# Gate product on VectorE, block copies on three engines and a step ahead of the convolution, gate and value steps side by side, in a two-layer encoder trunk

## The chip, the core and the metric

The kernel runs on one core of a Trainium2 chip. The core has five engines that each work through a queue of their own in order: TensorE (PE, with its weight loads as PEld), VectorE (DVE), ScalarE (ACT), GpSimd (POOL) and SyncE (SP), which issues most transfers. The metric is the time of one execution on the device in microseconds (us); lower is better.

## What is computed

The input is 256 positions of 2048 features in float32. Two layers follow each other: a mixer (grouped-query attention in layer 0, dilated windowed attention in layer 1) and a gated MLP with a convolution of width 3 over the positions between up-projection and activation. The change lies in the MLP, and in one table for the second mixer that is prepared beside the first MLP.

```python
D_FF = 5632
CONV_WIDTH = 3

def conv_ffn(h, w_up, conv_w, conv_b, w_down):
    u = h @ w_up                                  # [256, 2 * D_FF]
    c = u.shape[-1]
    u = lax.conv_general_dilated(u, conv_w[:, None, :].astype(u.dtype), window_strides=(1,),
                                 padding=((1, 1),), dimension_numbers=('NWC', 'WIO', 'NWC'),
                                 feature_group_count=c) + conv_b
    gate, val = jnp.split(u, 2, axis=-1)
    return (jax.nn.silu(gate) * val) @ w_down

def reference(x, ...):
    h = x
    for i in range(DEPTH):                        # 2 layers
        hn = rms_norm(h, mix_norm[i])
        h = h + (mixer_a(hn, ...) if i % 2 == 0 else mixer_b(hn, ..., rel_bias))
        h = h + conv_ffn(rms_norm(h, ffn_norm[i]), w_up[i], conv_w[i], conv_b[i], w_down[i])
    return rms_norm(h, final_norm)
```

## The kernel before

**Matrix products.** Every weight block of 128 x 1024 is loaded into one of six `raw` slots by SyncE (`feed`, `load_raw`). ScalarE rounds it to `wh` (line 120) and VectorE forms the remainder `wl` (line 121); these pairs lie in a ring of three slots, and four in the down-projection. The activations are split in the same way. A product is then three matmuls, high by high, high by low and low by high (lines 145 to 147), each with 512 columns. One weight block feeds 12 matmuls. This is called a step here, because `step()` is called after it.

**The up-projection.** `ffn` cuts the 5632 hidden features into 11 blocks of 512, in two halves of 6 and 5 (`HALVES`). For block p the kernel projects the gate block and then the value block: 8 steps each, a pair of 16 steps. What follows a projection is a generator, `up_post`, which `start` puts on the list `pending`. Each `step()` advances the oldest one to its next `yield`, so that its instructions are recorded between the matmuls of the following projection. The scheduler of the programming layer then sets the order on each engine; `wh` and `wl` are given priority there (`AHEAD`).

`up_post` has these pieces. ScalarE takes the projection out of the accumulators, scaled (`s`, line 420), and VectorE transposes each 32 x 32 block in place (`t`, line 421). Sixteen copies of 32 partitions x 256 elements then bring the blocks to their places in `u` (lines 425 to 436), so that positions lie along the free dimension. The string `PLACE` names the engine of each copy: p is GpSimd, a is ScalarE, any other letter is VectorE. Copies into the same 32 partitions are kept in sequence by semaphores. The convolution of each half block is one ScalarE instruction (line 441) and two on VectorE (lines 445 and 447) for each 128 features. For a gate, Silu follows. For a value, `glu` multiplies gate and value (line 455) and splits the product into the operands `ah` and `al` of the down-projection (lines 270 and 271).

**Blocks with sums.** The down-projection treats block 0 and block 2 of the first half and block 0 of the second (`SKG`) with seven products for eight, and so needs sums of their quarters. For these, `glu_forms` takes the place of `glu`: the same product (line 463), then more sums and splits. There are 6 such pairs in the two layers, and 16 plain ones.

**The down-projection** of a half follows its up-projection at once; the last value's `up_post` is worked off in its first steps. Sums of weight blocks (line 222) are made on VectorE.

**Bias lines.** The generator `bias_lines` is put on the list `spare` in layer 0. Six times it forms a line of biases by a matmul, copies it to `lnt` (line 883, two slots) and writes it to a scratch tensor in device memory with four transfers, issued by SyncE (line 886). `spare` is advanced only when `pending` is empty.

Of the kernel before, what the change touches and what calls it, by code (L numbers as in the profile page):

```python
# [10 lines left out]
ALU = mybir.AluOpType  # L11
# [11 lines left out]
NRAW, NHL = 6, 3  # L23
SKG = ((0, 2), (0,))
ORDER = (1, 2, 5, 3, 7, 6, 4)
PLACE = "pappaappapappapa"
AHEAD = 45
NWARM = 11

# [2 lines left out]
def tile_encoder(ctx: ExitStack, tc: tile.TileContext, x, xT, w_a, w_ao, q_gain, k_gain, w_b, w_bo,  # L32
                 rel_bias, gains, w_up, conv, w_down, final_norm, rope, ident_c, onehot, out):
    nc = tc.nc
# [45 lines left out]
    pending, spare = [], []  # L80

    def start(gen):
        if next(gen, StopIteration) is not StopIteration:
            pending.append(gen)

    def step():
        while pending:
            if next(pending[0], StopIteration) is not StopIteration:
                return
            pending.pop(0)  # L90
        if spare and next(spare[0], StopIteration) is StopIteration:
            spare.pop(0)

    def drain(keep=0):
        while len(pending) > keep:
            step()
# [279 lines left out]
    def ffn(l, hT, ss_in, g_next, last, side=None):  # L376
        with tc.tile_pool(name=nm("wpool"), bufs=1) as wp, tc.tile_pool(name=nm("fpool"), bufs=1) as fp:
# [35 lines left out]
            def up_post(acc, n, cs, after=None):  # L413
                u = us.pop(0)
                us.append(u)
                yield
                s = fp.tile([P, 2, 512], F32, tag="s", name=nm("s"))
                t = fp.tile([P, 2, 512], F32, tag="t", name=nm("t"))
                for m in range(2):
                    nc.scalar.activation(s[:, m], acc[m], AF.Copy, scale=rstd[:, m:m + 1])  # L420
                    nc.vector.transpose(t[:, m], s[:, m])  # L421
                yield
                tv = t.rearrange("p m (j q c) -> p j m q c", j=4, q=4)
                uv = u.rearrange("p j (m t) -> p j m t", m=2)
                for i in range(16):
                    if i == 8:
                        yield
                    a, b = i // 4, (i // 4 + i) % 4
                    dst = uv[32 * b:32 * b + 32, :, :, 32 * a:32 * a + 32]
                    src = tv[32 * a:32 * a + 32, :, :, b]  # L430
                    if PLACE[i] == "p":
                        nc.gpsimd.tensor_copy(dst, src)  # L432
                    elif PLACE[i] == "a":
                        nc.scalar.activation(dst, src, AF.Copy)  # L434
                    else:
                        nc.vector.tensor_copy(dst, src)
                for hh in range(2):
                    yield
                    c = cs[hh]
                    for j in range(2):  # L440
                        nc.scalar.activation(halves(c[:, j]), halves(u[:, 2 * hh + j])[:, :, :P], AF.Identity,
                                             bias=tap(n, 2 * hh + j, 3), scale=tap(n, 2 * hh + j, 1))
                    for j in range(2):
                        cj, uj = halves(c[:, j]), u[:, 2 * hh + j]
                        nc.vector.scalar_tensor_tensor(cj, halves(uj[:, :NT])[:, ::-1], tap(n, 2 * hh + j, 0), cj,  # L445
                                                       ALU.mult, ALU.add)
                        nc.vector.scalar_tensor_tensor(cj, halves(uj[:, 1:NT + 1])[:, ::-1], tap(n, 2 * hh + j, 2), cj,  # L447
                                                       ALU.mult, ALU.add)
                    if after is None:
                        nc.scalar.activation(c, c, AF.Silu)  # L450
                    else:
                        yield from after(hh)

            def glu(cg, cv, slots, k0):
                nc.gpsimd.tensor_tensor(cv, cg, cv, ALU.mult)  # L455
                yield
                for j in range(2):
                    split(*slots[k0 + j], cv[:, j, :])
# [1 line left out]
            kept = {}  # L460

            def glu_forms(cg, cv, fm, hh):
                nc.gpsimd.tensor_tensor(cv, cg, cv, ALU.mult)  # L463
                yield

                def put(p, src):
# [30 lines left out]
            for hf, (p0, p1) in enumerate(HALVES):  # L497
# [3 lines left out]
                def new_form():  # L501
                    pool, k = next(tags)
                    return tuple(pool.tile([P, NT], F32R, tag=f"a{c}{k}", name=nm("a" + c)) for c in "hl")

                for p in range(p0, p1):
                    if p - p0 in SKG[hf]:
                        fm = forms[p - p0] = {f: new_form() for f in (1, 7, 2, 5, 4, 6, 3) + (0,) * hf}
# [63 lines left out]
                        eng.dma_start(out.rearrange("(p m) c -> m p c", m=2)[m, :, n * 512:(n + 1) * 512], hs)  # L571

                np_ = p1 - p0
                drain(1)
                wd = w_down[l][:, p0:p1]
                if last and hf == 1:
# [287 lines left out]
    def bias_lines(wp, lp):  # L864
        if True:
# [9 lines left out]
            for b in range(6):  # L875
                for _ in range(2):
                    yield
                c0, w = ((0, 512), (512, 256), (768, 256))[b // 2]
                t = ps_tile()
                nc.tensor.matmul(t[:, :w], lh[:, 4 * b:4 * b + 4, :].rearrange("p a r -> p (a r)"),  # L880
                                 oh[:, c0:c0 + w], start=True, stop=True)
                ln = lnt[:, b % 2]
                nc.vector.tensor_copy(ln[:, :w], t[:, :w])
                dst = scr0[4 * b:4 * b + 4] if b < 2 else scr1[4 * (b - 2):4 * (b - 2) + 4]
                for i in range(4):
                    nc.sync.dma_start(dst[:, 32 * i:32 * i + 32, :], ln[:, :w])

    def mixer_b(hT, ss_in):
        with tc.tile_pool(name="bpool", bufs=1) as bp:
# [219 lines left out]
```

## Time and profile before

| what | value |
|---|---|
| median of 3 runs | 2330.32 us (2327.9 to 2332.01) |
| the profiled execution | 2330.72 us, span of its instructions 2328.9 us |
| granted TensorE clock, mean | 0.996 |
| PE, PEld busy | 2278.9 us, 1859.0 us |
| DVE, ACT, POOL busy | 1667.5 us, 1366.7 us, 388.4 us |
| HBM traffic | 429.20 MB read, 187 GB/s over the span |

The busy time of an engine is the time in which at least one of its instructions ran. In the views quoted below, a row of stretches has start and end in us, length, busy time of each engine with its number of instructions in brackets, the granted TensorE clock, the busy share of the DMA engines and GB/s. A row of the timeline has start and length in us, engine, line, operation, output and input; in square brackets stands how long the engine was idle before it, and who ended that. A group row ends with busy us and mean ns of one, then the idle time before them. Durations of instructions in a row on one engine can overlap a little.

### The profile page before, as it was taken

To read this page: it belongs to the slowest core of one execution; us is meant where nothing else is said; L and a number is where in the kernel's file an instruction comes from. 1 tells how busy PE (TensorE), PEld (TensorE's weight loads), DVE (VectorE), ACT (ScalarE), POOL (GpSimd) and SP (SyncE) were. 2 spreads that over 40 slices of the span, in tenths; PEclk is the share of its full clock that TensorE was granted. 3 is DMA by queue.
4 is the path that set the end of the run, shared out by engine and by line. 5 is a ranking of instruction groups with operands and counts; after the bars stand their busy time and mean duration, and the time that the engine had idled before them with its cause. 6 is when DMAs were issued, how large, how long until landed. Compare 5 with 4: busy or idle time off the path is not lost.

```text
span 2328.9 us, 28808 instructions
## 1 busy us (share of the span) xinstructions
PE 2278.9 (98%) x10169; PEld 1859.0 (80%) x10169; DVE 1667.5 (72%) x2301; ACT 1366.7 (59%) x2022; POOL 388.4 (17%) x524
## 2 busy tenths in 40 slices
PE   9999999999999999999999999999999999999998
PEld 7788777787787887788888888878778878878876
DVE  6877867667876667878776876575776688676684
ACT  6565467666546766455454454445767655567653
POOL 2210023233002333010000000001323210133230
PEclk9999999999999999999999999999999999999999
DMA  8445555665565564666655555555555556555663
GB/s 298 153 136 163 183 172 182 202 222 164 196 220 178 192 199 152 218 219 198 195 177 174 179 190 164 179 190 194 171 181 191 186 190 209 190 179 191 200 208 127
DMA packets 125136, 437.37 MB, mean 188 GB/s; under 512 B 13904, under 2 KB 16720, under 8 KB 124992
## 3 DMA queue, kind: packets, MB, share of 16 engines
q1 hardware_dynamic: 122912, 429.84, 56.6%
q0 software_dynamic: 1648, 5.15, 0.7%
q8 instruction: 79, 1.29, 0.2%
q14 instruction: 65, 0.53, 0.1%
q10 hardware_dynamic: 432, 0.56, 0.1%
HBM read 429.20 MB, written 6.29 MB: 187 GB/s over the span
## 4 chain that ended last, share of the span: by engine, by line
PE 72%; DVE 12%; POOL 7%; ACT 4%; issue 3%; DMA 3%; SPq 0%; DVEq 0%; POOLq 0%; ACTq 0%
PE acc L146 20%; PE acc L147 19%; PE acc L145 19%; DVE wl L121 5%; POOL u L432 4%; PE acc L258 4%; PE acc L253 3%; PE acc L255 3%; ACT wh L120 2%; POOL cv L455 2%; DVE tT L314 1%; DVE cv L445 1%; DVE cv L447 1%; POOL cv L463 1%; DMA raw<-in_w_up_dram 1%
## 5 line engine op out<-in xcount | busy, mean ns | idle before, releaser
L121 DVE TENSOR_TENSOR wl<-raw,wh 128x1024 fp32r<-128x1024 f32 x822 | 1005.4, 1230 | 449.9 <-ACT wh L120 446.0
L120 ACT ACTIVATE wh<-raw 128x1024 fp32r<-128x1024 f32 x822 | 862.3, 1057 | 608.1 <-PE acc L147 394.9
L146 PE MATMUL acc<-wl,xh 128*128 128x512 f32 x2176 | 855.6, 393 | 13.5 <-DVE wl L121 11.1
L145 PE MATMUL acc<-wh,xh 128*128 128x512 f32 x2176 | 854.6, 393 | 5.9 <-ACT wh L120 5.3
L147 PE MATMUL acc<-wh,xh 128*128 128x512 f32 x2176 | 850.2, 391 | 0.0
L146 PEld LDWEIGHTS acc<-wl,xh 128*128 128x128 f32 x2176 | 409.8, 188 | 115.5 <-DVE wl L121 32.2
L145 PEld LDWEIGHTS acc<-wh,xh 128*128 128x128 f32 x2176 | 410.2, 189 | 93.0 <-ACT wh L120 8.4
L147 PEld LDWEIGHTS acc<-wh,xh 128*128 128x128 f32 x2176 | 409.7, 188 | 83.9
L432 POOL COPY u<-t 32x256 f32<-32x256 f32 x396 | 213.9, 540 | 827.7 <-DVE t L421 806.8
L253 PE MATMUL acc<-wh,ah 128*128 128x512 f32 x524 | 205.5, 392 | 6.7 <-ACT wh L120 6.5
L255 PE MATMUL acc<-wh,al 128*128 128x512 f32 x524 | 204.3, 390 | 0.0
L146 PE MATMUL acc<-wl,ah 128*128 128x512 f32 x480 | 187.9, 392 | 1.9 <-DVE wl L121 1.7
L145 PE MATMUL acc<-wh,ah 128*128 128x512 f32 x480 | 187.4, 390 | 0.0
L147 PE MATMUL acc<-wh,al 128*128 128x512 f32 x480 | 187.0, 390 | 0.0
L434 ACT ACTIVATE u<-t 32x256 f32<-32x256 f32 x308 | 129.2, 420 | 52.3 <-POOL u L432 27.5
L258 PE MATMUL acc<-wl,ah 128*128 128x512 f32 x524 | 148.4, 394 | 8.2 <-DVE wl L121 8.0
L258 PEld LDWEIGHTS acc<-wl,ah 128*128 128x128 f32 x524 | 96.7, 188 | 35.9 <-DVE wl L121 16.5
L253 PEld LDWEIGHTS acc<-wh,ah 128*128 128x128 f32 x524 | 98.3, 188 | 32.3 <-ACT wh L120 11.5
L255 PEld LDWEIGHTS acc<-wh,al 128*128 128x128 f32 x524 | 98.4, 188 | 20.3
L146 PEld LDWEIGHTS acc<-wl,ah 128*128 128x128 f32 x480 | 90.2, 188 | 23.9 <-DVE wl L121 5.7
L147 PEld LDWEIGHTS acc<-wh,al 128*128 128x128 f32 x480 | 90.1, 188 | 18.5
L145 PEld LDWEIGHTS acc<-wh,ah 128*128 128x128 f32 x480 | 90.2, 188 | 18.3
(168 smaller groups left out, 1596.1 us busy)
## 6 DMA issues: line engine op xcount, KB each, us to landing
raw<-in_w_up_dram SPq DMA_DIRECT2D x352, 512.0 KB
raw<-in_w_down_dram SPq DMA_DIRECT2D x176, 512.0 KB
raw<-in_w_b_dram SPq DMA_DIRECT2D x144, 512.0 KB
raw<-in_w_bo_dram SPq DMA_DIRECT2D x48, 512.0 KB
raw<-in_w_a_dram SPq DMA_DIRECT2D x40, 512.0 KB
raw<-in_w_ao_dram SPq DMA_DIRECT2D x32, 512.0 KB
raw<-in_w_a_dram SPq DMA_DIRECT2D x16, 256.0 KB
h<-in_x_dram SPq DMA_DIRECT2D x4, 512.0 KB
```

Source lines behind the costliest of these rows:

```text
L120: nc.scalar.activation(wh, r, AF.Copy)
L121: nc.vector.tensor_tensor(wl, r, wh.bitcast(F32), ALU.subtract)
L145: nc.tensor.matmul(accs[m], xh, wh[:, j, :], start=st, stop=False)
L146: nc.tensor.matmul(accs[m], xh, wl[:, j, :], start=False, stop=False)
L147: nc.tensor.matmul(accs[m], xl, wh[:, j, :], start=False, stop=sp)
L253: nc.tensor.matmul(acc[k], xh, wh[:, j, :], start=k in fresh, stop=False)
L255: nc.tensor.matmul(acc[k], xl, wh[:, j, :], start=False, stop=False)
L258: nc.tensor.matmul(acc[k], xh, wl[:, j, :], start=False, stop=last[k] == i and j == 1)
L314: nc.vector.transpose(o[cols].rearrange("p a (m t) -> p a m t", m=2)[:, :, :, rows], s[rows].rearrange("p m (a c) -> p a m c", c=P)[:, :, ...
L432: nc.gpsimd.tensor_copy(dst, src)
L434: nc.scalar.activation(dst, src, AF.Copy)
L455: nc.gpsimd.tensor_tensor(cv, cg, cv, ALU.mult)
```

## The change

The product of gate and value moves from GpSimd to VectorE, in both `glu` and `glu_forms`. `PLACE` gives 5 copies of each projection to GpSimd (9 before), 3 to ScalarE (7 before) and 8 to VectorE (none before). The `yield` between copies 7 and 8 moves behind copy 15: all 16 copies are recorded in one step and none in the next, ahead of the convolution. While the list `wide` is not empty, that is from the start of a half's up-projection until all of its projections are recorded, `step()` advances the two oldest generators of `pending`, not one, and `spare` as well when fewer than two are pending. The bias writes are issued by GpSimd and not by SyncE, with one more `yield` ahead of them.

```diff
-PLACE = "pappaappapappapa"
+PLACE = "pvavpvpvavpvpvav"
...
+    wide = []
+
     def step():
-        while pending:
+        if wide:
+            for g in pending[:2]:
+                if next(g, StopIteration) is StopIteration:
+                    pending.remove(g)
+        while pending and not wide:
             if next(pending[0], StopIteration) is not StopIteration:
                 return
             pending.pop(0)
-        if spare and next(spare[0], StopIteration) is StopIteration:
+        if spare and len(pending) < 2 and next(spare[0], StopIteration) is StopIteration:
             spare.pop(0)
...
                 for i in range(16):
-                    if i == 8:
-                        yield
                     a, b = i // 4, (i // 4 + i) % 4
...
                         nc.vector.tensor_copy(dst, src)
+                yield
                 for hh in range(2):
...
             def glu(cg, cv, slots, k0):
-                nc.gpsimd.tensor_tensor(cv, cg, cv, ALU.mult)
+                nc.vector.tensor_tensor(cv, cg, cv, ALU.mult)
...
             def glu_forms(cg, cv, fm, hh):
-                nc.gpsimd.tensor_tensor(cv, cg, cv, ALU.mult)
+                nc.vector.tensor_tensor(cv, cg, cv, ALU.mult)
...
+                wide.append(1)
                 for p in range(p0, p1):
...
                 np_ = p1 - p0
+                wide.clear()
                 drain(1)
...
                 dst = scr0[4 * b:4 * b + 4] if b < 2 else scr1[4 * (b - 2):4 * (b - 2) + 4]
+                yield
                 for i in range(4):
-                    nc.sync.dma_start(dst[:, 32 * i:32 * i + 32, :], ln[:, :w])
+                    nc.gpsimd.dma_start(dst[:, 32 * i:32 * i + 32, :], ln[:, :w])
```

The line numbers of the changed kernel are higher, by 6 from `split_raw` on: 126 and 127 are the splits `wh` and `wl`, 427 the transposes, 436, 438 and 440 the copies on GpSimd, ScalarE and VectorE, 446, 450 and 452 the convolution, 460 and 468 the product, 276 and 277 the splits `ah` and `al`, 894 the bias writes.

ScalarE before, after the value projection of a plain pair (p = 4 of layer 0), from the block copies to the splits of the product; `cv` is the value after the convolution, and the brackets name the engines waited for:

```order
L434 ACTIVATE u_2607<-t_4639 32x8x32 [waits Pool_49]
L434 ACTIVATE u_2607<-t_4639 32x8x32 [waits Activation_49]
L120 ACTIVATE wh_4723<-raw_4719 128x1024 [waits DMAHW7_49,PE_49]
L434 ACTIVATE u_2607<-t_4639 32x8x32 [waits Activation_49]
L441 ACTIVATE cv_4216<-u_2607,cw_2594 128x256 [waits Activation_49,Pool_49]
L441 ACTIVATE cv_4216<-u_2607,cw_2594 128x256
L441 ACTIVATE cv_4217<-u_2607,cw_2594 128x256
L120 ACTIVATE wh_4743<-raw_4720 128x1024 [waits DMAHW0_49,PE_49]
L441 ACTIVATE cv_4217<-u_2607,cw_2594 128x256
L270 ACTIVATE ah_4206<-cv_4216 128x256 [waits Pool_49]
L270 ACTIVATE ah_4208<-cv_4216 128x256 [waits DVE_49]
L120 ACTIVATE wh_4770<-raw_4766 128x1024 [waits DMAHW5_49,PE_49]
```

ScalarE now, at the same place:

```order
L438 ACTIVATE u_2607<-t_4639 32x8x32 [waits DVE_49] x3
L126 ACTIVATE wh_4723<-raw_4719 128x1024 [waits DMAHW3_49,PE_49]
L446 ACTIVATE cv_4230<-u_2607,cw_2594 128x256 [waits DVE_49,Pool_49]
L446 ACTIVATE cv_4230<-u_2607,cw_2594 128x256
L446 ACTIVATE cv_4231<-u_2607,cw_2594 128x256 x2
L126 ACTIVATE wh_4743<-raw_4720 128x1024 [waits DMAHW4_49,PE_49]
L126 ACTIVATE wh_4770<-raw_4766 128x1024 [waits DMAHW5_49,PE_49]
L276 ACTIVATE ah_4220<-cv_4230 128x256 [waits DVE_49]
L276 ACTIVATE ah_4222<-cv_4230 128x256
```

The first split `ah` waits for VectorE and no longer for GpSimd, and the weight split `wh_4770`, which stood behind it, stands ahead of it. The three copies wait for VectorE each.

VectorE before, at the same place, from the second transpose on:

```order
L421 STREAM_TRANSPOSE t_4639<-s_4638 128x512 [waits Activation_49]
L121 TENSOR_TENSOR wl_4697<-raw_4669,wh_4696 128x1024 [waits DMAHW6_49,Activation_49]
L121 TENSOR_TENSOR wl_4724<-raw_4719,wh_4723 128x1024 [waits DMAHW7_49,DVE_49,Activation_49]
L445 SCALAR_TENSOR_TENSOR cv_4216<-u_2607,cw_2594,cv_4216 128x256 [waits Activation_49] x2
L447 SCALAR_TENSOR_TENSOR cv_4216<-u_2607,cw_2594,cv_4216 128x256 [waits DVE_49] x2
```

VectorE now:

```order
L427 STREAM_TRANSPOSE t_4639<-s_4638 128x512 [waits Activation_49]
L440 COPY u_2607<-t_4639 32x8x32 [waits DVE_49]
L440 COPY u_2607<-t_4639 32x8x32
L440 COPY u_2607<-t_4639 32x8x32 [waits Pool_49] x3
L127 TENSOR_TENSOR wl_4697<-raw_4677,wh_4696 128x1024 [waits DMAHW2_49,Activation_49]
L440 COPY u_2607<-t_4639 32x8x32 [waits Activation_49]
L440 COPY u_2607<-t_4639 32x8x32 [waits Pool_49]
L440 COPY u_2607<-t_4639 32x8x32 [waits Activation_49]
L127 TENSOR_TENSOR wl_4724<-raw_4719,wh_4723 128x1024 [waits DMAHW3_49,Activation_49]
```

Five copies, three of them with a wait for GpSimd, now stand ahead of the weight remainder `wl_4697`, and three more between it and `wl_4724`.

SyncE before, at the first bias writes (`scr` is the scratch tensor, `raw` a weight block of the up-projection):

```order
L137 DMA raw_3909<-in_w_up_dram 128x1024 [waits DMAHW5_49,DVE_49]
L886 DMA scr_97<-lnt 4x32x512 [waits DVE_49,Pool_49]
L886 DMA scr_97<-lnt 4x32x512
L886 DMA scr_97<-lnt 4x32x512 [waits DMAHW6_49]
L886 DMA scr_97<-lnt 4x32x512 [waits DMAHW7_49]
L137 DMA raw_3910<-in_w_up_dram 128x1024 [waits DMAHW0_49,DVE_49]
```

GpSimd now, at the third line of biases:

```order
L436 COPY u_2606<-t_3635 32x8x32 [waits DVE_49] x3
L894 DMA scr_98<-lnt 4x32x256 [waits DMASW5_49,DVE_49]
L436 COPY u_2606<-t_3635 32x8x32 [waits DVE_49]
L894 DMA scr_98<-lnt 4x32x256 [waits DMASW6_49]
L894 DMA scr_98<-lnt 4x32x256 [waits DMASW7_49]
L436 COPY u_2606<-t_3635 32x8x32 [waits DVE_49]
```

The weight loads no longer have the bias writes ahead of them on SyncE; the writes, with their waits for earlier writes and for the line, now stand between block copies on GpSimd.

## The prediction

> **What bounds the kernel now.** I read the page first, then the busy time by stretches, then the timelines of the stretches that fall short.
>
> ```profile
> PE 2278.9 (98%) x10169; PEld 1859.0 (80%) x10169; DVE 1667.5 (72%) x2301; ACT 1366.7 (59%) x2022; POOL 388.4 (17%) x524
> ```
>
> TensorE (PE) is the bound, and the change takes no matmul away. Only its gaps can be won. The stretches, 22 us each (columns: stretch, length, PE busy with the matmuls in brackets, granted clock, DMA share, GB/s), show where they are:
>
> ```profile
> 312.00:334.00 22.00, 22.00 (x98) 1.00 0.56 181
> 334.00:356.00 22.00, 18.68 (x71) 0.92 0.45 150
> 422.00:444.00 22.00, 17.40 (x66) 0.84 0.66 232
> 576.00:598.00 22.00, 18.01 (x76) 1.00 0.58 199
> 752.00:774.00 22.00, 21.12 (x91) 1.00 0.56 183
> 906.00:928.00 22.00, 21.17 (x91) 1.00 0.31 105
> 928.00:940.00 12.00, 9.72 (x39) 1.00 0.61 176
> 1648.00:1670.00 22.00, 18.84 (x79) 1.00 0.49 161
> 1736.00:1758.00 22.00, 21.20 (x92) 1.00 0.54 168
> 1868.00:1890.00 22.00, 18.79 (x78) 1.00 0.56 176
> 2046.00:2068.00 22.00, 21.05 (x90) 1.00 0.53 169
> 2222.00:2244.00 22.00, 19.93 (x79) 1.00 0.64 198
> ```
>
> A full stretch holds 98 matmuls, so one is 22/98 = 0.2245 us. The other rows are short by 27, 32, 22, 7, 7, 14 (39 where 12 us hold 53), 19, 6, 20, 8 and 19: 181, or 40.6 us. That is nearly all there is to win. A pair in the middle of a phase loses next to nothing (columns PE, PEld, DVE, ACT, POOL):
>
> ```profile
> 820.25:842.35 22.10, 21.96 (x97) 17.84 (x96) 13.95 (x22) 15.13 (x25) 9.34 (x11) 1.00 0.58 186
> 842.35:864.46 22.11, 22.11 (x98) 18.05 (x97) 16.06 (x20) 15.90 (x25) 4.48 (x9) 1.00 0.63 202
> ```
>
> Three kinds of place lose time. First, pair 0 of each layer (334 and 1648), here in layer 0:
>
> ```profile
> 344.12 2.21 POOL L463 TENSOR_TENSOR cv<-cg,cv 128x512 f32<-128x512 f32 x1 [4.51 <-DVE cv L447]
> 346.37 0.73 ACT L270 ACTIVATE ah<-cv 128x256 fp32r<-128x256 f32 x2 [4.09 <-POOL cv L463]
> 347.57 1.04 ACT L120 ACTIVATE wh<-raw 128x1024 fp32r<-128x1024 f32 x1
> 348.79 1.18 DVE L121 TENSOR_TENSOR wl<-raw,wh 128x1024 fp32r<-128x1024 f32 x1
> 348.00:349.00 1.00, 0.35 (x2) 1.00 0.16 61
> 349.00:350.00 1.00, 0.16 (x1) 1.00 0.00 0
> 351.00:352.00 1.00, 1.00 (x4) 0.50 0.52 184
> ```
>
> ScalarE stands 4.09 us at a split that waits for GpSimd's product. The weight split `wh` is queued behind it, `wl` waits for `wh`, and PE runs dry for 1.5 us and then at half clock. Second, the ends of the halves (576, 928, 1868, 2222) have the same wait, longer:
>
> ```profile
> 579.18 3.35 POOL L455 TENSOR_TENSOR cv<-cg,cv 128x512 f32<-128x512 f32 x1 [5.63 <-DVE cv L447]
> 582.56 0.72 ACT L270 ACTIVATE ah<-cv 128x256 fp32r<-128x256 f32 x2 [2.68 <-POOL cv L455]
> 579.00:580.00 1.00, 0.40 (x2) 1.00 0.68 221
> 583.00:584.00 1.00, 0.00 (x0) 1.00 0.54 217
> ```
>
> Third, 422 is a queue: SyncE spends 10.18 us on four bias writes, the weight loads stand behind them, and ScalarE waits 7.20 us for weights.
>
> ```profile
> 413.62 10.18 SPq L886 DMA_DIRECT2D scr<-lnt  x4
> 436.45 1.06 ACT L120 ACTIVATE wh<-raw 128x1024 fp32r<-128x1024 f32 x1 [7.20 <-DMA raw<-in_w_up_dram]
> 435.00:436.00 1.00, 0.00 (x0) 0.81 0.95 389
> ```
>
> **The change part by part.** Prices come from these rows (groups: busy us, mean ns; tile view: minimum, median, maximum in ns; timeline; waits: us in total, times, longest):
>
> ```profile
> L455 POOL TENSOR_TENSOR cv<-cg,cv 128x512 f32<-128x512 f32 x32 | 77.7, 2429 | 111.2 <-DVE cv L447 111.2
> L606 DVE TENSOR_TENSOR h<-h,cu 128x512 f32<-128x512 f32 x6 | 4.1, 686 | 0.0
> L832 DVE TENSOR_SCALAR pr<-pr,l 128x256 f32<-128x256 f32 x32 | 9.9, 351 | 0.6
> L314 DVE STREAM_TRANSPOSE tT<-h 32x256 f32<-32x256 f32 x144 | 62.8, 436 | 2.6
> L432 POOL COPY u<-t x396: 391/401/1482, 315.9 to 2220.2; 32x256 f32<-32x256 f32 x198
> 561.15 7.69 POOL L432 COPY u<-t 32x256 f32<-32x256 f32 x9 [19.32 <-DVE t L421]
> 823.94 5.07 POOL L432 COPY u<-t 32x256 f32<-32x256 f32 x9 [16.25 <-DVE t L421]
> L434 ACT ACTIVATE u<-t 32x256 f32<-32x256 f32 x308 | 129.2, 420 | 52.3 <-POOL u L432 27.5 <-DVE t L421 18.4
> ACT cv L441 <- POOL u L432: 7.0, 6, 1.6
> 828.70 1.38 DVE L121 TENSOR_TENSOR wl<-raw,wh 128x1024 fp32r<-128x1024 f32 x1 [2.73 <-ACT wh L120]
> L906 POOL DMA_DIRECT2D bt<-scr x8 | 6.1, 764 | 151.6 <-DMA raw<-in_w_b_dram 88.1 <-DVE lg L946 63.5
> ```
>
> *Gate product to VectorE (DVE).* A product of 512 elements with both inputs in SBUF takes DVE 0.69 us (L606) against GpSimd's 2.21 to 3.35. ScalarE's wait falls by 1.5 us at a pair 0 and by 2.7 at an end, and in the new order the second split of `wh` stands ahead of the first `ah`. The gap at 348 goes in both layers (1 - 0.35 + 1 - 0.16 = 1.5 us each), in layer 0 with the half clock behind it (0.92 in the mean, 0.08 x 22 = 1.8 us): 4.8 us. The rest of the 46 x 0.2245 = 10.3 us lost at the two places I credit by a third, 1.7: 6.5 us, between 3 (the next DVE work is late instead) and 9. At an end the two rows of 579 and 583 alone show PE standing 0.6 and 1.0 us, of 22 x 0.2245 = 4.9 us lost in that stretch; 2.66 us saved covers them and the edges of their neighbours. I take 2 us each, 8 for four, between 4 and 10; next late there is the load of `w_down`. The four weak rows 752, 906, 1736 and 2046 are short by 28 matmuls, 6.3 us; none need be due to the product alone: 2.5, between 0 and 5.
>
> *Bias writes to GpSimd's queue.* Weight loads no longer stand behind 24 writes: 7.2 us are lost at 422, I take 6 back, between 4 and 7. The writes now stand among GpSimd's block copies, four at a time: 4 x 0.764 = 3.1 us (L906 is the nearest row). DVE copies that wait for a block copy behind them, and the `wl` behind those, pay for it. `spare` now also runs beside one pending generator, so the six lines come sooner, in busier steps. The extra `yield` lets the line copy end first. I take +2, between 0 and 6.
>
> *Block copies.* Per projection GpSimd has 5 instead of 9, ScalarE 3 instead of 7, DVE 8 instead of none. No row shows this copy on DVE. The nearest is L832 (one SBUF input, 256 elements): 0.35 us; bounds 0.25 (below it, since instructions in a row overlap) and 0.44 (L314, 32 rows). I take 0.35 as the same element count without a transpose. A pair then adds 16 x 0.35 + 2 x 0.69 = 7.0 us to DVE's 13.95 + 16.06 = 30.0: 37.0 of 44.2. DVE runs in order, and its copies wait for GpSimd's: copies into the same 32 partitions are kept in sequence. I put 1 us of standing on each projection, 39.0 in all. It still fits, but not at each moment: behind the fifth copy stands `wl`. The `wl` of 828.70 ends at 830.08; PE, at 12 matmuls (2.72 us) a step from 820.25, needs it four steps on, at 831.1, so 1.0 us is spare. Five copies ahead of the `wl` before it and three ahead of it, with the standing, and a third ScalarE copy that waits until after that `wl`, use this up. I charge 0.3 us to each of 16 plain pairs and 0.6 to each of the 6 with the extra sums: 4.8 + 3.6 = +8.4, between 0 (all absorbed) and +33 (1.5 us a pair, see the first rival). ScalarE gets 8 x 0.42 = 3.4 us a pair less, which costs nothing and wins nothing: it isn't full.
>
> The Trainium skill (page "SBUF — State Buffer", section "Who interferes with whom") says that a VectorE copy in two-port mode, or a VectorE instruction with two SBUF inputs, and a GpSimd instruction that reads SBUF shut each other out for a whole instruction. The trace agrees for the second case: GpSimd's copy has a median of 0.40 us and a maximum of 1.48, about one `wl` longer. By that rule the copies would take turns, and the sum would be that of the first rival.
>
> *A step earlier, side by side.* All 16 copies are issued in one step and an empty step follows. No engine gets more work, and the convolution's wait (7.0 us in all between `cv` and the GpSimd copies) may go. A gate needs 5 of 8 steps, so gate and value overlap only at pair 0 and after the pairs with sums: 0 by itself, since DVE's bursts grow as the backlog shrinks.
>
> **Sum.** -6.5 - 8 - 2.5 - 6 + 2 + 8.4 = -12.6 us. The profiled execution took 2330.72 us (span 2328.9); it would take 2318.1. The median, 2330.32, is 0.4 lower: 2318 us forecast.
>
> **The rivals.**
>
> *DVE becomes the bound (slower).* Place: the copies ahead of `wl` in each projection. If each GpSimd copy has to wait for a DVE instruction, as at 561.15 (7.69/9 = 0.85 us), and DVE stands through them, a projection costs DVE 8 x 0.35 + 5 x 0.85 = 7.05 us, where I have 3.8. A pair is then 30.0 + 1.4 + 14.1 = 45.5 us of 44.2: 1.3 us over, 29 for 22 pairs. In place of 8.4 the sum is -12.6 + 20.6 = +8: 2338 us. It decides where copies and standing exceed (44.2 - 31.4)/2 = 6.4 us a projection. For it: DVE and GpSimd meet more often at a higher DVE load. Against it: nine copies in the pair at 820 needed only 5 us with ScalarE's seven between them. Chance 0.26.
>
> *All covers hold.* The waits cost nothing (0 instead of 8.4) and the product gives its upper bounds at ends and weak rows (10 and 5): 2318 - 8.4 - 4.5 = 2305 us. For it: 7 us of DVE idle time remain in a pair. Chance 0.15.
>
> *Transfers take the place of the product.* If a late weight is next at the ends and at pair 0, only half of 6.5, 8 and 2.5 comes: 2318 + 8.5 = 2327 us. For it: the DMA share of 0.45 at 334 is low only because slots are released late; against it, the waits above name the product, not a load. Chance 0.12.
>
> **How the numbers follow.** The forecast has 0.47. A measurement of this kernel can tell about 0.2% (4.7 us) from no change. Faster: 0.47 + 0.15 + 0.02 of the transfers = 0.64; same 0.10; slower 0.26. The range goes from 2300 (the second rival, with 9 at pair 0, and the queue's 7) to 2340 (the first rival, with 2 us to spare); beyond lie the dearer half of that rival, and less than 0.05 below. The forecast's own range is 2308 to 2325.
>
> **What would show it.** Right: no ScalarE wait for a product above 1 us; no weight wait near 422; about 90 or more matmuls in the rows 334, 422, 1648; DVE near 37 us in a plain pair, PE still at 97. Wrong: plain pairs longer than 45 us with PE waiting for `wl`; DVE copies above 0.44 us, or standing 2 us and more at GpSimd copies; gaps at the ends unchanged with DMA named as releaser.

## The result, and the profile after

The changed kernel takes 2296.64 us (median of 4 runs, 2294.5 to 2300.27), the kernel before 2330.93 on the same chip: ratio 0.9857, interval 0.9839 to 0.9874. The gain is 33 to 34 us. Forecast was 2318 us, from 2300 to 2340. The direction was right, the size less than half, and the time lies 3.4 us below the range. The profiled execution took 2300.27 us, its span is 2298.5.

TensorE is still the bound. On the page of the changed kernel it is busy 15.3 us less with the same 10169 matmuls, since matmuls that run late or at half clock count with their longer time:

```profile
PE 2263.6 (98%) x10169; PEld 1863.5 (81%) x10169; DVE 1808.1 (79%) x2697; ACT 1296.6 (56%) x1846; POOL 227.5 (10%) x328
```

The stretches of 22 us of the changed kernel at the places that the prediction named (columns: stretch, length, PE busy with the matmuls in brackets, granted clock, DMA share, GB/s). It reaches the places behind the first a little sooner than the kernel before:

```profile
264.00:286.00 22.00, 16.19 (x63) 0.84 0.58 186
330.00:352.00 22.00, 21.34 (x93) 1.00 0.54 169
396.00:418.00 22.00, 20.09 (x79) 0.92 0.81 256
572.00:594.00 22.00, 20.68 (x90) 1.00 0.59 200
902.00:924.00 22.00, 20.20 (x88) 1.00 0.45 151
1562.00:1584.00 22.00, 19.12 (x89) 1.00 0.54 172
1628.00:1650.00 22.00, 21.10 (x92) 1.00 0.55 174
```

Pair 0 went from 71 and 79 matmuls to 93 and 92 (330 and 1628), the first end of a half from 76 to 90 (572). The bias lines moved from 422 to 396 and still lose time. The starts of the two FFNs (264 and 1562) are a loss that is larger or new; before, the first of them read

```profile
264.00:286.00 22.00, 19.82 (x85) 0.92 0.63 201
```

The plain pair of the prediction, in the same two windows of the changed kernel (PE, PEld, DVE, ACT, POOL), has gained as well:

```profile
820.25:842.35 22.10, 22.10 (x99) 18.34 (x98) 19.85 (x34) 14.33 (x23) 3.16 (x5) 1.00 0.62 195
842.35:864.46 22.11, 22.11 (x99) 18.31 (x99) 17.44 (x27) 14.20 (x19) 3.17 (x5) 1.00 0.62 196
```

VectorE has 19.85 + 17.44 = 37.3 us there, where 37.0 was forecast, and yet TensorE holds 99 + 99 matmuls instead of 97 + 98. The groups of the changed kernel (busy us, mean ns, idle time ahead and its releaser):

```profile
L440 DVE COPY u<-t 32x256 f32<-32x256 f32 x352 | 125.6, 357 | 15.7 <-ACT u L438 5.7
L436 POOL COPY u<-t 32x256 f32<-32x256 f32 x220 | 141.2, 642 | 1044.1 <-DVE t L427 1016.2 <-DVE u L440 21.0
L276 ACT ACTIVATE ah<-cv 128x256 fp32r<-128x256 f32 x84 | 30.9, 410 | 58.9 <-DVE cv L460 43.0 <-DVE cv L468 15.9
L460 DVE TENSOR_TENSOR cv<-cg,cv 128x512 f32<-128x512 f32 x32 | 22.1, 690 | 0.4
```

The prices were right: 357 ns for a copy (0.35 us forecast) and 690 ns for a product (0.69). VectorE's standing at its copies is 15.7 us over 44 projections, 0.36 us each, where 1 us was taken.

To place the gain, the times at which the k-th matmul ends were compared between traces, and the differences grouped by place. On the clock of the kernel before, the FFN starts are 267 to 314 and 1577 to 1622 us, pair 0 is the 52 us behind each, the bias lines go on from there to 456, and an end of a half is its down-projection. Columns: the change; each part alone on the kernel before; and the three parts without the stepping. Microseconds against the profiled run of before, minus is sooner:

```
place                       change  product  copies  writes  stepping  no stepping
starts of the two FFNs        +7.9     -2.5    -2.1    -2.9      +6.4         -1.9
pair 0, both layers           -8.8     -5.4    -3.0    -0.1      -0.9         -9.4
bias lines (layer 0)          -3.7     -0.4    +1.6    -5.3      +7.3         -8.1
other up-projection pairs    -10.2    -12.1   +12.0    +3.4      -0.2        -10.1
ends of the four halves      -15.7    -12.9    +1.4    +2.5      +3.6        -12.6
rest                          -0.4     -0.1    +0.2     0.0      +0.2         +1.0
sum                          -30.9    -33.5   +10.0    -2.4     +16.4        -41.0
```

The 2 to 3 us at the FFN starts in the columns without the stepping are most likely a loss of that one profiled run of before and no gain of a part, since four kernels with different parts show them alike. The "rest" is how far single runs differ where the kernels are alike.

**What stands at the FFN start.** The timeline of the changed kernel, and three stretches of 1 us:

```profile
277.14 0.41 PE L399 MATMUL ps<-ident,cr 128*128 128x128 f32 x2 [2.77 <-POOL rb L877]
280.62 0.42 PE L399 MATMUL ps<-ident,cr 96*128 96x96 f32 x1 [2.83 <-DMA cr<-in_conv_dram]
281.07 0.53 DVE L400 COPY cw<-ps 128x352 f32<-128x352 f32 x1 [6.61 <-PE ps L399]
281.55 1.06 ACT L126 ACTIVATE wh<-raw 128x1024 fp32r<-128x1024 f32 x1 [8.35 <-PE acc L153]
```

```profile
279.00:280.00 1.00, 0.00 (x0) 0.50 0.90 359
281.00:282.00 1.00, 1.00 (x6) 0.50 0.01 4
285.00:286.00 1.00, 1.00 (x4) 0.63 0.68 193
```

The three transposes of the convolution's taps (L399) now stand between the projection's first matmuls and ahead of the late transposes of `h` (L347), since the stepping advances the taps' generator beside the older one. The taps come in two loads, which land at 276.8 and 280.6; TensorE stands 2.77 us ahead of the first and 2.83 us ahead of the second, then runs at half clock until after 285. (The memset `rb` that the first row names had ended before that load landed, at 276.5.)

**What stands at the bias lines.** The writes are off SyncE's queue, and no weight load is waited for between 396 and 445 (before: 7.2 us). But the copy of a line into `lnt`, which has two slots, now waits on VectorE for the write two lines earlier, with a `wl` and the end of a convolution behind it (timeline of the changed kernel):

```profile
409.90 0.42 DVE L890 COPY lnt<-ps 128x256 f32<-128x256 f32 x1 [2.48 <-DMA scr<-lnt]
411.89 0.63 ACT L455 ACTIVATE cg<-cg 128x512 f32<-128x512 f32 x1 [5.17 <-DVE cg L452]
411.52 0.50 PE L152 MATMUL acc<-wl,xh 128*128 128x512 f32 x1 [1.81 <-DVE wl L127]
```

### The profile page after: what moved, and what is told of

It is laid out like the page before. It is cut to its first block, busy times and chain, and to the rows that moved or that the text cites. A ratio compares the mean times of both kernels' runs of the same rounds, so it can differ in the third digit from the quotient of the medians.

```text
span 2298.5 us, 28788 instructions
## 1 busy us (share of the span) xinstructions
PE 2263.6 (98%) x10169; PEld 1863.5 (81%) x10169; DVE 1808.1 (79%) x2697; ACT 1296.6 (56%) x1846; POOL 227.5 (10%) x328
## 4 chain that ended last, share of the span: by engine, by line
PE 80%; DVE 13%; issue 3%; DMA 2%; ACT 1%; POOL 1%; SPq 0%; DVEq 0%; POOLq 0%; ACTq 0%
PE acc L152 21%; PE acc L153 21%; PE acc L151 21%; DVE wl L127 6%; PE acc L264 5%; PE acc L261 4%; PE acc L259 4%; DVE tT L320 1%; DVE u L440 1%; ACT wh L126 1%; DMA scr<-lnt 1%; DVE al L277 1%; DVE cv L450 1%; PE ps L291 1%; DVE t L427 1%
## 5 line engine op out<-in xcount | busy, mean ns | idle before, releaser
L436 POOL COPY u<-t 32x256 f32<-32x256 f32 x220 | 141.2, 642 | 1044.1 <-DVE t L427 1016.2
L440 DVE COPY u<-t 32x256 f32<-32x256 f32 x352 | 125.6, 357 | 15.7 <-ACT u L438 5.7
L261 PEld LDWEIGHTS acc<-wh,al 128*128 128x128 f32 x524 | 98.4, 188 | 20.5
L438 ACT ACTIVATE u<-t 32x256 f32<-32x256 f32 x132 | 55.2, 418 | 97.9 <-DVE u L440 85.6
```

What stands on the lines that cost most here:

```text
L261: nc.tensor.matmul(acc[k], xl, wh[:, j, :], start=False, stop=False)
```

## The experiments

All times below stand against 2328.9 to 2329.4 us of the kernel before in the same batch. A difference from the kernel before in us is the ratio less 1, times 2329. A difference between two changed kernels is that of their medians; formed from the ratios, some come out up to 2.5 us larger or smaller, and no conclusion below hangs on that.

### One part alone

**The product alone.** It was measured in two batches; the trace is from the second.

```diff
-                nc.gpsimd.tensor_tensor(cv, cg, cv, ALU.mult)      # glu and glu_forms
+                nc.vector.tensor_tensor(cv, cg, cv, ALU.mult)
```

> The kernel before with the gate product alone moved to VectorE. The prediction's sum gives this part -6.5 - 8 - 2.5 = -17 us (-7 to -24) and leaves plain pairs at 195 matmuls per 44 us. The product theory, formed on the trace of the changed kernel, says that the GpSimd product also cost a little in every plain pair (ScalarE's split waits for it, the weight split stands behind): then about -25 to -32 us, with plain pairs at 197 to 198 matmuls. The copy theory, by which plain pairs gained because the block copies end sooner on three engines, expects -12 to -20 us and plain pairs unchanged.

> The gate product alone on VectorE once more, for a readable trace. Product theory: 2297 us again, plain pairs at 197 to 198 matmuls per 44 us, no ScalarE wait for a product above 1 us, and the loss at 422 (7 us weight wait) still there. If plain pairs stay at 195, the product's gain lies at the ends of the halves alone.

Measured: 2297.06 us (0.9856, 0.984 to 0.9871), again 2296.56 us (0.9862, 0.9847 to 0.9876), that is -32 to -33.5 us. This one line alone brings as much as the whole change. The waits of ScalarE's splits for a product (us in total, times, longest), before and then with the product alone:

```profile
ACT ah L270 <- POOL cv L455: 77.3, 32, 3.2
```

```profile
ACT ah L270 <- DVE cv L455: 31.4, 26, 1.9
```

A stretch of 44 us among the plain pairs, before and then with the product alone:

```profile
814.00:858.00 44.00, 43.86 (x193) 1.00 0.60 196
```

```profile
814.00:858.00 44.00, 44.00 (x196) 1.00 0.61 192
```

A plain pair of before thus lost 3 matmuls, 0.67 us. Its timeline shows how. The split waits for GpSimd's product, the two `wh` behind it end late, the first of the two `wl` ends only at 843.2, and the matmuls around it start 0.29 and 0.34 us apart instead of 0.23:

```profile
840.24 0.73 ACT L270 ACTIVATE ah<-cv 128x256 fp32r<-128x256 f32 x2 [3.24 <-POOL cv L455]
840.87 1.99 ACT L120 ACTIVATE wh<-raw 128x1024 fp32r<-128x1024 f32 x2
841.95 2.36 DVE L121 TENSOR_TENSOR wl<-raw,wh 128x1024 fp32r<-128x1024 f32 x2 [0.50 <-ACT wh L120]
842.94 0.39 PE L145 MATMUL acc<-wh,xh 128*128 128x512 f32 x1
843.23 0.50 PE L146 MATMUL acc<-wl,xh 128*128 128x512 f32 x1
843.57 0.40 PE L147 MATMUL acc<-wh,xh 128*128 128x512 f32 x1
```

The other product of the pair does the same 6 us earlier, with 0.52 and 0.34 us. With the product on VectorE neither gap is left.

**The block copies alone.**

```diff
-PLACE = "pappaappapappapa"
+PLACE = "pvavpvpvavpvpvav"
```

> The kernel before with the block copies alone shared by three engines (5 GpSimd, 3 ScalarE, 8 VectorE of 16). The prediction: +8.4 us (0 to +33), VectorE near 35 us of a plain pair, weight splits late behind its copies. The product theory: within 3 us of no change, since the product is still on GpSimd and is what the splits wait for. The copy theory: -8 to -15 us, plain pairs at 197 to 198 matmuls per 44 us.

Measured: 2340.41 us (1.0042, 1.0028 to 1.0055), +9.8 us. The prediction's +8.4 holds here, and its place: the plain pairs, by 12.0 us in the table. The second transpose and the convolution of one gate projection in the timeline of before, and then with the copies shared, there with the two late matmuls of the pair:

```profile
845.96 0.70 DVE L421 STREAM_TRANSPOSE t<-s 128x512 f32<-128x512 f32 x1
852.67 0.87 DVE L445 SCALAR_TENSOR_TENSOR cg<-u,cw,cg 128x256 f32<-128x256 f32 x2
```

```profile
846.83 0.70 DVE L421 STREAM_TRANSPOSE t<-s 128x512 f32<-128x512 f32 x1
854.00 0.87 DVE L445 SCALAR_TENSOR_TENSOR cg<-u,cw,cg 128x256 f32<-128x256 f32 x2
837.94 0.50 PE L146 MATMUL acc<-wl,xh 128*128 128x512 f32 x1 [0.29 <-DVE wl L121]
844.10 0.50 PE L146 MATMUL acc<-wl,xh 128*128 128x512 f32 x1 [0.43 <-DVE wl L121]
```

The waits with the copies shared:

```profile
ACT ah L270 <- POOL cv L455: 108.1, 32, 5.3
```

From the end of the second transpose to the convolution it takes 6.0 us before and 6.5 with the shared copies; for a value it is 6.1 and 6.5. The product on GpSimd, which follows the value, starts and ends 0.4 us later, the splits wait 108.1 instead of 77.3 us, and both gaps of the pair open further.

**The bias writes alone.**

```diff
-                for i in range(4):
-                    nc.sync.dma_start(dst[:, 32 * i:32 * i + 32, :], ln[:, :w])
+                yield
+                for i in range(4):
+                    nc.gpsimd.dma_start(dst[:, 32 * i:32 * i + 32, :], ln[:, :w])
```

> The kernel before with the 24 bias writes alone moved to GpSimd's queue (with the extra yield after each line copy). The prediction: -6 + 2 = -4 us (-7 to +2), no weight wait of 7 us near 422. If the writes slow the weight loads by their share of the DMA engines rather than by standing ahead of them in SyncE's queue, 0 to -2 us, with the loss moved and not gone.

Measured: 2329.05 us (11 runs; 0.9996, 0.9987 to 1.0005): no difference. In the one profiled run the place itself gains 5.3 us, near the 6 forecast, and 5.9 us are lost later: 3.3 in the rest of the first half's up-projection, where the later lines are written, and 2.5 at the ends. GpSimd's products are still there; that the writes delay them was not shown singly.

**The stepping alone** (`wide`, all 16 copies in one step, the rule of `spare`).

```diff
+        if wide:
+            for g in pending[:2]:
+                if next(g, StopIteration) is StopIteration:
+                    pending.remove(g)
...
-        if spare and next(...
+        if spare and len(pending) < 2 and next(...
```

> The kernel before with the stepping alone changed: gate and value steps side by side, all 16 copies in one step ahead of the convolution, bias lines also beside one pending step. The prediction: 0 us. The theory of the early transposes, formed on the trace of the changed kernel: the three transposes of the taps come before the two late transposes of the FFN start, TensorE stands there for the taps' load, +4 to +8 us for both layers together, with fewer than 70 matmuls in 264:286.

Measured: 2351.03 us (1.0086, 1.0073 to 1.0099), +20 us: not 0, and dearer than the theory of the early transposes said. The FFN starts cost what that theory said (64 matmuls in 264:286). About as much is lost at the bias lines, where SyncE still writes (timeline, SPq is its queue):

```profile
403.25 6.91 SPq L893 DMA_DIRECT2D scr<-lnt  x4
410.91 0.42 DVE L890 COPY lnt<-ps 128x256 f32<-128x256 f32 x1 [8.85 <-DMA scr<-lnt]
412.52 0.80 PE L152 MATMUL acc<-wl,xh 128*128 128x512 f32 x1 [6.54 <-DVE wl L127]
```

The lines now follow each other so closely that VectorE stands 8.85 us for a slot of `lnt`, `wl` waits behind it, and TensorE stands 6.54 us.

### Pairs and threes

The four parts alone add up to -32 + 9.8 - 1 + 20 = -3 us, and the change brings -33. So parts change each other's price. Three kernels hold the product and the writes, and nothing, the stepping or the copies beside them.

Product and writes on the kernel before:

```diff
-                nc.gpsimd.tensor_tensor(cv, cg, cv, ALU.mult)
+                nc.vector.tensor_tensor(cv, cg, cv, ALU.mult)
...
+                yield
                 for i in range(4):
-                    nc.sync.dma_start(dst[:, 32 * i:32 * i + 32, :], ln[:, :w])
+                    nc.gpsimd.dma_start(dst[:, 32 * i:32 * i + 32, :], ln[:, :w])
```

> The kernel before with the product on VectorE and the bias writes on GpSimd's queue, nothing else. The parts add: 2297 - 1 = 2296 us. If the bias writes cost their gain at GpSimd's products alone (a write ahead of a product), which are gone here: 2290 to 2293 us. If the change needs the copies or the stepping for its gain, above 2297 us.

Product, writes and stepping, that is the changed kernel with the old sharing:

```diff
-PLACE = "pvavpvpvavpvpvav"
+PLACE = "pappaappapappapa"
```

> The changed kernel with the old sharing of the block copies (9 GpSimd, 7 ScalarE). The prediction's +8.4 us for copies on VectorE would make this 8 us faster than the changed kernel: 2288 us. The copies alone cost 9.7 us in the kernel before, where the product was still on GpSimd. If they compete with the product for one path (VectorE work ahead of a product that the split waits for), moving the product removes that cost too: 2294 to 2300 us. If the shorter copy chain helps once the product is gone: 2300 to 2310 us.

Product, writes and copies, that is the changed kernel with the old stepping:

```diff
-        if wide:
-            for g in pending[:2]:
-                if next(g, StopIteration) is StopIteration:
-                    pending.remove(g)
-        while pending and not wide:
+        while pending:
...
-        if spare and len(pending) < 2 and next(...
+        if spare and next(...
...
                 for i in range(16):
+                    if i == 8:
+                        yield
```

> The changed kernel with the old stepping (no side by side, the yield in the middle of the copies, bias lines beside no pending step). The prediction: no difference. The theory of the early transposes and of the denser bias lines: the losses at 264:286 (5 us more than before), 1562:1584 (3 us) and 396:418 (3 to 4 us) go: 2284 to 2290 us, with at least 85 matmuls in 264:286 and 1 or 2 less in 572:594. If side by side is what filled the plain pairs, 2300 us or more.

Measured: 2292.71 us (0.9844, 0.9829 to 0.9859), 2304.39 us (0.9901, 0.9884 to 0.9917) and 2287.01 us (0.9821, 0.9806 to 0.9836).

- The writes are worth 4 us once the product is off GpSimd (2296.56 to 2292.71).
- The copies, which cost 9.8 us beside a product on GpSimd, win 5.7 us without the stepping (2292.71 to 2287.01) and 7.8 us with it (2304.39 to 2296.64). The sign turned.
- The stepping costs 11.7 us without and 9.6 us with the shared copies. The changed kernel would be faster without this part.

Why the sign turns is seen in two places. At pair 0 of layer 0, the timeline with product and writes, and then with the copies shared too:

```profile
325.83 0.70 DVE L421 STREAM_TRANSPOSE t<-s 128x512 f32<-128x512 f32 x1
333.22 0.49 DVE L445 SCALAR_TENSOR_TENSOR cv<-u,cw,cv 128x256 f32<-128x256 f32 x1 [0.94 <-ACT cv L441]
```

```profile
327.37 0.70 DVE L421 STREAM_TRANSPOSE t<-s 128x512 f32<-128x512 f32 x1
333.58 0.87 DVE L445 SCALAR_TENSOR_TENSOR cv<-u,cw,cv 128x256 f32<-128x256 f32 x2
```

The value's convolution starts 6.7 us after the transpose in the first and 5.5 us in the second. That chain is what pair 0 waits for, and each layer gains 2.0 us there by the traces. In a plain pair the convolution still comes 0.4 us later with the copies, but the product takes 0.7 us and not 2.4. It ends 10.5 us behind the value's second transpose on the kernel before, 10.8 with the copies, 9.9 with the product on VectorE and 10.3 with both. So the delay by the copies hides: by the traces they cost the other pairs 1.0 us here, against 12.0 on the kernel before. A stretch of plain pairs with product, writes and copies:

```profile
814.00:858.00 44.00, 44.00 (x195) 1.00 0.60 194
```

TensorE is busy throughout.

### One part undone

The changed kernel with the product back on GpSimd, and with the writes back on SyncE:

```diff
-                nc.vector.tensor_tensor(cv, cg, cv, ALU.mult)
+                nc.gpsimd.tensor_tensor(cv, cg, cv, ALU.mult)
```

```diff
-                yield
                 for i in range(4):
-                    nc.gpsimd.dma_start(dst[:, 32 * i:32 * i + 32, :], ln[:, :w])
+                    nc.sync.dma_start(dst[:, 32 * i:32 * i + 32, :], ln[:, :w])
```

> The changed kernel with the gate product back on GpSimd. If the parts add as measured one by one on the kernel before (+9.7 copies, -1.0 bias writes, +20.4 stepping): 2358 us, that is 61 us slower than the changed kernel. If copies and stepping cost the same 2 or 3 places (one covers the other), 2340 to 2350 us. If the prediction's -17 for the product held inside the change, 2314 us.

> The changed kernel with the bias writes back on SyncE's queue. The prediction's -6 + 2 for that part and the 3.9 us measured with the product on VectorE: 2300.5 us. In the stepping alone on the kernel before, the bias lines cost 13 us near 420, twice what they cost in the kernel before; if SyncE's queue is why, the writes are worth more here: 2303 to 2310 us.

Measured: 2340.22 us (1.0042, 1.0027 to 1.0058) and 2311.5 us (0.9921, 0.9904 to 0.9939). Without the product's move the change is slower than before, by 9.8 us; the product is worth 43 us inside it. The costs of copies, stepping and writes don't simply add (that would be 2358). By the traces the kernel is better than the sum of these parts by 8 us at the bias lines and by 12 us at the ends of the halves; why, was not followed at the ends. The writes are worth 15 us inside the change, more than was expected, because the stepping makes the lines dense; with SyncE as their queue 396:418 falls to 54 matmuls, and a line copy waits again (timeline with the writes on SyncE):

```profile
406.40 0.42 DVE L890 COPY lnt<-ps 128x256 f32<-128x256 f32 x1 [8.14 <-DMA scr<-lnt]
```

### The taps put off

```diff
             def taps_gen():
-                yield
+                for _ in range(8):
+                    yield
                 taps()
```

> The changed kernel with the three transposes of the taps put off by seven more steps (some 76 PE instructions later), nothing else. If what the stepping costs at the start of each FFN is TensorE standing for the taps' load: -9 us against the changed kernel (6.5 in layer 0, 3.8 in layer 1, a little given back), 2286 to 2289 us, at least 85 matmuls in 264:286, while 396:418 stays at about 79. If the loss there comes from other work moved by the stepping, above 2293 us.

> The three parts without the stepping (product, copies, bias writes), with the taps put off as well. That kernel still waits 1.7 us for the taps' load at 281.8: -2 us in layer 0 and up to -1 in layer 1, 2284 to 2285 us. If the next work is late instead: 2287 us, no change.

Measured: on the changed kernel 2286.4 us (0.9818, 0.9805 to 0.9832), 10.2 us faster, as the theory of the early transposes said; without the stepping 2287.36 us (0.9823, 0.9809 to 0.9836), no change. Three stretches of the first:

```profile
264.00:286.00 22.00, 21.79 (x99) 17.37 (x98) 13.67 (x21) 12.60 (x20) 4.23 (x9) 1.00 0.61 204
396.00:418.00 22.00, 21.51 (x94) 17.22 (x93) 18.47 (x31) 14.29 (x21) 9.87 (x15) 1.00 0.91 290
1562.00:1584.00 22.00, 22.00 (x102) 18.18 (x101) 11.55 (x13) 9.26 (x11) 0.00 (x0) 1.00 0.55 180
```

The starts of both FFNs are full. That 396:418 rose from 79 to 94 had not been expected: most of the loss at the lines went without any change to them. The lines fall elsewhere against the work beside them; which of the things that moved did it was not tried.

**Side by side at the ends only**, taps put off, old rule of `spare`.

```diff
-                wide.append(1)
                 for p in range(p0, p1):
+                    if p == p1 - 2:
+                        wide.append(1)
...
-        if spare and len(pending) < 2 and next(...
+        if spare and not pending and next(...
```

> The changed kernel with the taps put off, side by side only in the last two pairs of a half, and bias lines beside no pending step, as before. If side by side wins 4 us at the first end of a half (matmul 2548) and loses at the FFN starts and the bias lines alone, this keeps the gain and drops the losses: 2279 to 2283 us. If the gain at that end needs side by side from the first pair on, 2284 to 2287 us.

Measured: 2285.64 us (5 runs; 0.9815, 0.9802 to 0.9829). It beats the kernel before by 43 us and the changed kernel by 11, but not the 2279 to 2283 of the expectation. At the first end of a half, where the full stepping has 5.3 us by the trace, this one has 3.2, so part of that gain seems to need side by side from further back. It can't be told apart from the 2286.4 and 2287.0 of its neighbours.

### All copies on VectorE

```diff
-PLACE = "pappaappapappapa"      # with product on VectorE and writes on GpSimd
+PLACE = "vvvvvvvvvvvvvvvv"
```

> Product and bias writes moved, and all 16 block copies of a projection on VectorE. It decides the prediction's first rival: VectorE then has 30.0 + 1.4 + 32 x 0.357 = 42.8 us of work in a plain pair of 44.2 without any standing. By the prediction's threshold (copies and standing over 6.4 us a projection; here 5.7 and no standing for other engines) it just fits in the mean, but behind the copies the weight splits come late: 0.65 us or more per pair, at least 15 us slower than the 2292.7 us with no copies on VectorE. If VectorE's load doesn't count at all below 100%: within 5 us of 2292.7.

Measured: 2308.5 us (0.9915, 0.9902 to 0.9929), 15.8 us slower than with none. The size fits, the place doesn't. The group of the copies:

```profile
L436 DVE COPY u<-t 32x256 f32<-32x256 f32 x704 | 200.9, 285 | 19.7
```

A stretch of plain pairs in it (PE, PEld, DVE, ACT, POOL), and the first end of a half (PE alone):

```profile
814.00:858.00 44.00, 44.00 (x195) 36.41 (x194) 40.26 (x77) 25.90 (x35) 0.00 (x0) 1.00 0.60 192
550.00:572.00 22.00, 18.05 (x75) 0.99 0.39 127
```

The same end with product and writes and no copy on VectorE:

```profile
550.00:572.00 22.00, 19.64 (x83) 1.00 0.44 146
```

With VectorE 40.3 us busy of 44 a plain pair loses nothing at all, though the convolution there comes 8.7 us behind the transposes and not 6.1. Of the 15.4 us between the two traces, 9.5 lie at the ends of the halves and 2.8 at pair 0 and the steps after it. The waits of the down-projection's matmuls for `wl` (us in total, times, longest), without copies on VectorE and then with all of them there:

```profile
PE acc L258 <- DVE wl L121: 7.4, 9, 1.6
```

```profile
PE acc L258 <- DVE wl L121: 13.6, 16, 1.9
```

So the weight splits do come late, as expected, but at the ends. A later convolution isn't the reason at the first end: it begins 8.4 us behind the transposes in both kernels. What holds `wl` up there was not followed further.

## Why the prediction was wrong, point by point

- **"A pair in the middle of a phase loses next to nothing."** This step failed, and most of the miss with it. 97 + 98 matmuls were read as full; with the product alone 44 us hold 196 in place of 193. The listed weak rows were taken for "nearly all there is to win", and the product was credited -2.5 us outside pair 0 and the ends. The product alone won 12.1 us in those pairs. With the copies' +8.4 the sum has +5.9 us there; the change measured -10.2, and that is 16 of the 18 us by which the trace undercuts the sum.
- **Block copies, +8.4 us.** This term failed too: right on the kernel before (+9.8), wrong in the change (-5.7 to -7.8). It was worked out with the 1.0 us of spare time that the `wl` of 828.70 had while the product was still on GpSimd, and added to a sum that had just taken that product away. The 37.0 us of VectorE work (37.3) and the copy's 0.35 us (357 ns) were right; the 1 us of standing per projection was 0.36. That the copies shorten the chain at pair 0 by 1.2 us was not looked at.
- **Gate product at pair 0 and the ends, -6.5 and -8.** The mechanism was right, the ends mis-sized: -5.4 and -12.9 with the product alone, -8.8 and -15.7 in the change (of pair 0, the copies brought 4.0). The upper bound of -10 was too low for the ends; that the two rows priced there show only part of what lies behind one late split is the likely reason. (A third of the 5.5 us left at pair 0 is 1.8, not 1.7.)
- **Bias writes, -6 + 2.** -5.3 at the place, and 0 in the time by themselves; -4 once the product is gone from GpSimd. In the change the place has -3.7, as forecast, but as -8.1 by the other parts and +4.4 by the denser stepping.
- **A step earlier, side by side, 0.** Wrong: +9.6 us in the change. "No engine gets more work" is true and is not the point. The stepping also advanced `taps_gen` and the lines, whose transfers were not due; the sum looked at `up_post` alone.
- **The signs to look for.** No ScalarE wait for a product above 1 us: wrong, the splits still wait 58.9 us in all (the group of L276) and up to 2.0 at once, but in the plain pairs that no longer reaches TensorE. No weight wait near 422: right. About 90 matmuls in the rows 334, 422 and 1648: 93, 79, 92 (the 79 at 396, where the lines now lie). VectorE near 37 us with TensorE at 97: right, and 99.
- **The rivals.** VectorE as the bound fell: even 40.3 us of 44 cost a plain pair nothing. "All covers hold" (2305) was nearest; the copies were covered as it said, and it too left the plain pairs out. Transfers taking the product's place is not seen.

The Trainium skill (page "SBUF — State Buffer", section "Who interferes with whom") has two kinds of VectorE instructions and GpSimd's reads shut each other out: copies in two-port mode, and instructions with two SBUF inputs. The traces agree for the second kind alone. In the changed kernel 45 of GpSimd's 220 copies take 1.2 us or more, and all of them meet a `wl`; before, 58 of 396 did, 54 of them beside a `wl` and 4 beside another VectorE instruction with two inputs. That larger share, 20% against 15%, is the main reason why their mean went from 540 to 642 ns. The 168 copies that meet only VectorE copies take at most 0.53 us; whether VectorE's copies run in two-port mode, no run tells. By that rule as the prediction used it, the time would have been 2338 us; it was 2296.64.

## What to carry to other kernels

When a change removes a wait and adds work near it, price the work against the slack that is left after the wait is gone; here the same copies cost 9.8 us with the wait and won 6 to 8 without it. Test whether a "full" stretch is full by what it holds elsewhere: three matmuls missing in every plain pair were a third of the gain. And when the order of generators changes, follow each one on the list, the small ones that wait for a load above all: undoing or delaying that part of this change gave 10 us more.

## What the runs showed of the hardware

At 264:286 of the changed kernel TensorE stood 5.6 us in two pieces, and its granted clock was 0.50 from 279 until after 285 though matmuls ran without a gap from 281: some 4.4 us at half speed, which by an estimate from these numbers lost 2.2 us on top of the standing. The Trainium skill (page "TensorE: Matmul & The Clock Gate", section "Part 1: The HAM clock gate (the "warmup" mystery)") says that the full clock comes back after a busy window of about 3.4 us, and that these windows run freely of the work; here it took 4.4, which fits. At 550:572 of the kernel with product and writes TensorE is idle for 2.4 us of 22 in all, and the clock stayed at 1.00.

A copy of 32 x 256 float32 elements takes VectorE 378 ns in the mean when a GpSimd copy runs at the same time (268 of the 352 in the changed kernel), and 288 when none does; in the kernel without GpSimd copies it takes 285. GpSimd's copies take 0.40 us in the median with and without VectorE copies beside them, at most 0.53 beside VectorE copies alone, and 1.2 us or more in 45 cases, each beside a `wl`.
